# A running minimum over 256 MB on one core: fewer correction passes, doubling steps in the serial middle, smaller pieces at the stage borders

## The chip, the core and the metric

The kernel runs on 1 core of one Trainium2 chip. The metric is device time in microseconds (us), the median over runs. The granted clock in the records is 1.0. A profile is one execution; its span is 1.8 to 2.3 us shorter than the time of the same execution, so stages are compared with stages and times with times.

A few names: HBM is the memory that holds the input and the output, SBUF the one that holds the tiles, with up to 128 partitions in the profile's lines; the profile's DMA lines move data between the two. In the profile PE is the matmul engine TensorE (used here for transposes), DVE is VectorE, ACT is ScalarE, POOL is GpSimd, which issues the gathers and scatters, and SPq is the queue that issues the loads and stores.

## The reference

```python
def setup_inputs():
    return {"x": np.random.randn(8192, 8192).astype(np.float32)}

def reference(x):
    return np.minimum.accumulate(x.flatten()).reshape(x.shape).astype(np.float32)
```

The output is the running minimum over all 67 million values in row order. On random data a new minimum is rare. Cut into 65,536 blocks of 1024 values, only 9 blocks of this draw hold a value below everything before them; every other block of the output is one constant.

## The kernel before

`x` is seen as 64 groups of 128 rows (one row per partition), each row as 8 blocks of 1024. The kernel works in four stages.

1. Load every group (4 MB) and reduce each block to its minimum.
2. In the middle, with no data moving, turn the 65,536 block minima into exclusive prefix minima `pfx`. This is done along the row (8 blocks), across the 128 rows of a group (after a transpose), and across the 64 groups. Each is a "windowed" reduction: an access pattern with overlapping windows, so that 128 results over windows of 128 make 16,384 element reads.
3. ScalarE (ACT) fills 128x1024 pieces with the constant `pfx`, and the tiles are stored. Beside that, the blocks that may hold a new minimum ("candidates", at most 16 per partition, padded with fillers) are gathered from HBM, and VectorE (DVE) scans them.
4. After the last store, the scanned candidate blocks are scattered over the output, 128 blocks at a time.

```python
    NCAND = 16
    ...
    with tc.tile_pool(name="xin", bufs=3) as xpool:
        for g in range(G):
            xt = xpool.tile([P, K, S], f32, tag="x")
            nc.sync.dma_start(out=xt, in_=xg[g])
            nc.vector.tensor_reduce(out=bmpad[:, g, K : 2 * K], in_=xt, axis=AX, op=MIN)
    ...
    win_x = bass.AP(tensor=tpad.tensor, offset=tpad.offset, ap=[tpad.ap[0], [1, P], [1, P]])
    nc.vector.tensor_reduce(out=xgt, in_=win_x, axis=AX, op=MIN)      # one of three windowed minima
    ...
    nc.vector.max(m1, score)                                          # 8 best candidates
    nc.vector.match_replace(out=score2, in_to_replace=m1, in_values=score, imm_value=-1.0)
    nc.vector.max(m2, score2)                                         # 8 more
    ...
    for i in range(NCAND):                                            # prefix of each candidate
        nc.gpsimd.indirect_dma_start(out=pgath[:, i : i + 1], ..., in_=pdram, ...)
    ...
        pwork = fixpool.tile([P, 2 * S], f32)                         # and qwork, with two memsets
        for i in range(NCAND):
            nc.gpsimd.indirect_dma_start(out=pwork[:, S : 2 * S], ..., in_=xflat, ...)
            # ten doubling steps of 128x1024 on VectorE, into fixres[:, i, :]
        for g in range(G):
            ot = opool.tile([P, K, S], f32, tag="o")
            for k in range(K):
                nc.scalar.activation(out=ot[:, k, :], in_=ones_s, ..., scale=pfx[:, g, k : k + 1])
            nc.sync.dma_start(out=og[g], in_=ot)
        for i in range(NCAND):
            nc.gpsimd.indirect_dma_start(out=oflat, ..., in_=fixres[:, i, :], in_offset=None)
```

## Time and profile before

Median 1382.05 us (12 runs, 1381.89 to 1382.38).

| stage | from | to | length, us |
|---|---|---|---|
| load, to the end of the last reduction | 0 | 632.2 | 632.2 |
| middle, to the end of `pfx` | 632.2 | 663.5 | 31.3 |
| stores, to the start of the first scatter | 663.5 | 1319.85 | 656.3 |
| scatters and end | 1319.85 | 1380.3 | 60.5 |

The first view is the windows of the kernel before. Each line gives a stretch in us from the start, its length, the busy time and instruction count of each engine, the clock, the busy share of the DMA engines and their GB/s.

```profile
core 0: us, PE busy (x) PEld busy (x) DVE busy (x) ACT busy (x) POOL busy (x), PEclk, DMA share, GB/s
0.00:623.50 623.50, 0.00 (x0) 0.00 (x0) 547.89 (x67) 0.00 (x0) 3.70 (x12) 1.00 1.00 431
623.50:663.50 40.00, 1.23 (x4) 0.51 (x4) 38.77 (x14) 0.00 (x0) 0.00 (x0) 1.00 0.00 0
663.50:674.00 10.50, 0.00 (x0) 0.00 (x0) 5.09 (x16) 10.40 (x10) 1.76 (x2) 1.00 0.35 25
674.00:1319.00 645.00, 0.00 (x0) 0.00 (x0) 196.92 (x160) 529.17 (x504) 42.44 (x31) 1.00 1.00 429
1319.00:1380.30 61.30, 0.00 (x0) 0.00 (x0) 0.00 (x0) 0.00 (x0) 15.42 (x16) 1.00 0.33 137
```

The two long stretches have the DMA engines fully busy at about 430 GB/s. The three other stretches, 112 us together, have them idle, or busy for about a third. That is where most of the time can be had.

The next view is the timeline around the middle: start, duration, engine, line, operation, and in brackets the idle time before it and what ended it.

```profile
623.50 8.69 DVE L71 TENSOR_REDUCE bmpad<-xt 128x8 f32<-128x8192 f32 x1 [0.98 <-DMA xt<-in_x_dram]
632.82 4.41 DVE L84 TENSOR_REDUCE E<-bmpad 128x512 f32<-128x4096 f32 x1
637.58 0.91 DVE L212 MEMSET pwork<- 128x1024 f32 x1 [0.16 <-issue]
638.42 17.15 DVE L95 TENSOR_REDUCE xgt<-tpad 64x128 f32<-64x16384 f32 x1
656.94 4.41 DVE L107 TENSOR_REDUCE tpf<-tp_pad 1x64 f32<-1x4096 f32 x1
662.83 0.69 DVE L122 TENSOR_TENSOR pfx<-E,rowpre 128x512 f32<-128x512 f32 x1
673.33 62.30 SPq L253 DMA_DIRECT2D out_dram<-ot  x8
```

The last tile's whole 8.69 us reduction comes after its data has landed, and one windowed reduction of 17.15 us is over half of the middle. The first store is issued 9.8 us after `pfx` is done (the last line sums eight store issues; only its start counts here).

The last view is the timeline of the scatters (three of sixteen).

```profile
1319.85 0.99 POOL L256 DMA_INDIRECT out_dram<-fixres,bidx  x1 [179.99 <-DMA out_dram<-ot]
1323.43 0.97 POOL L256 DMA_INDIRECT out_dram<-fixres,bidx  x1 [2.60 <-DMA out_dram<-fixres,bidx]
1327.05 0.96 POOL L256 DMA_INDIRECT out_dram<-fixres,bidx  x1 [2.64 <-DMA out_dram<-fixres,bidx]
```

Each scatter waits for the one before it to land; all write the same tensor. The median gap from start to start is 3.56 us. The last two gaps are 4.05 us; they are about 0.5 us longer than the others, and nothing here tells why.

### The profile page before, as it was taken

Reading aid. Unit: us, or ns where it says so; the run is one execution under the profiler, and the core shown is the slowest. Engines: PE = TensorE matmul, PEld = TensorE weight load, DVE = VectorE, ACT = ScalarE, POOL = GpSimd, SP = SyncE. Lnnn points to the kernel's source line nnn. Section 1 sums busy time; section 2 is a strip of 40 time slices with the busy share of each in tenths; the row PEclk is TensorE's granted clock in tenths of the full one; section 3 lists DMA queues with packets and bytes.
Section 4 is the critical chain, followed back from the end, with each engine's and each line's share of the span. In section 5 each row is a group of like instructions: output and inputs, shape, how many; then the busy total and the mean of one; then the engine's idle time right before and its main releaser. Section 6 shows DMA issues by size and latency. Waiting matters only on the chain.

```text
span 1380.3 us, 1251 instructions
## 1 busy us (share of the span) xinstructions
PE 1.2 (0%) x4; PEld 0.5 (0%) x4; DVE 788.7 (57%) x255; ACT 539.6 (39%) x513; POOL 63.3 (5%) x60
## 2 busy tenths in 40 slices
PE   0000000000000000000000000000000000000000
PEld 0000000000000000000000000000000000000000
DVE  5989889898988889899324333554333553000000
ACT  0000000000000000000798878888888788888500
POOL 1000000000000000000400000001000000000022
DMA  9999999999999999990599999999999999999933
GB/s 410 427 439 428 438 429 437 430 436 432 434 432 433 434 432 436 430 438 4 205 423 436 426 435 431 439 426 439 430 433 430 437 428 438 427 439 427 438 151 137
DMA packets 31770, 554.01 MB, mean 401 GB/s; under 512 B 11280, under 2 KB 11280, under 8 KB 15376
## 3 DMA queue, kind: packets, MB, share of 16 engines
q1 hardware_dynamic: 26640, 537.14, 90.5%
q0 software_dynamic: 5120, 16.79, 3.0%
q14 instruction: 10, 0.08, 0.0%
HBM read 276.83 MB, written 277.09 MB: 401 GB/s over the span
## 4 chain that ended last, share of the span: by engine, by line
DMA 67%; DVE 16%; ACT 15%; issue 2%; POOL 0%; ACTq 0%; POOLq 0%; PE 0%
DMA out_dram<-ot 33%; DMA xt<-in_x_dram 32%; ACT ot L246 15%; DVE bmpad L71 14%; DMA out_dram<-fixres,bidx 2%; DVE xgt L95 1%; POOL out_dram L256 0%; DVE tpf L107 0%; DVE E L84 0%; ACT L246 0%; POOLq L287 0%; ACTq L287 0%; DVE qwork L213 0%; DVE pwork L212 0%; DVE pfx L122 0%
## 5 line engine op out<-in xcount | busy, mean ns | idle before, releaser
L71 DVE TENSOR_REDUCE bmpad<-xt 128x8 f32<-128x8192 f32 x64 | 555.9, 8686 | 74.7 <-DMA xt<-in_x_dram 74.7
L246 ACT ACTIVATE ot<-ones_s,pfx 128x1024 f32<-128x1024 f32 x512 | 538.3, 1134 | 95.3 <-DMA out_dram<-ot 95.3
L235 DVE TENSOR_TENSOR qwork<-pwork 128x1024 f32<-128x1024 f32 x80 | 98.0, 1225 | 299.4 <-DMA pwork<-in_x_dram,bidx 297.2
L246 ACT ACT_TABLE_LOAD x1 | 1.3, 1283 | 663.6 <-DVE pfx L122 663.6
L235 DVE TENSOR_TENSOR pwork<-qwork 128x1024 f32<-128x1024 f32 x64 | 78.4, 1225 | 2.2
L216 POOL DMA_INDIRECT pwork<-in_x_dram,bidx x16 | 28.9, 1805 | 419.2 <-DVE qwork L235 418.9
L199 POOL DMA_INDIRECT pgath<-pdram,bidx x16 | 15.3, 957 | 672.2 <-DMA pdram<-pfx 667.7
L256 POOL DMA_INDIRECT out_dram<-fixres,bidx x16 | 15.4, 964 | 219.9 <-DMA out_dram<-ot 180.0
L226 DVE SCALAR_TENSOR_TENSOR fixres<-qwork,pgath 128x1024 f32<-128x1024 f32 x16 | 20.6, 1285 | 0.6
L95 DVE TENSOR_REDUCE xgt<-tpad 64x128 f32<-64x16384 f32 x1 | 17.2, 17153 | 0.0
L107 DVE TENSOR_REDUCE tpf<-tp_pad 1x64 f32<-1x4096 f32 x1 | 4.4, 4408 | 0.0
L84 DVE TENSOR_REDUCE E<-bmpad 128x512 f32<-128x4096 f32 x1 | 4.4, 4408 | 0.0
L64 DVE MEMSET bmpad<- 128x512 f32 x1 | 0.5, 485 | 0.9 <-PEq L276 0.9
L213 DVE MEMSET qwork<- 128x1024 f32 x1 | 0.9, 912 | 0.2 <-issue 0.2
L212 DVE MEMSET pwork<- 128x1024 f32 x1 | 0.9, 912 | 0.2 <-issue 0.2
L48 POOL MEMSET ones_s<- 128x1024 f32 x1 | 1.0, 956 | 0.0
L87 PE MATMUL mt_ps<-identity,rowmin 128*64 128x128 f32 x1 | 0.4, 392 | 633.0 <-DVE rowmin L76 633.0
L50 POOL IOTA bmap_i<- 128x512 int32 x1 | 0.8, 756 | 0.0
L143 DVE TENSOR_TENSOR score<-sc,sc 128x512 f32<-128x512 f32 x1 | 0.7, 693 | 0.1
L153 DVE MAX8 m<-score 128x8 f32<-128x512 f32 x1 | 0.7, 694 | 0.0
L141 DVE TENSOR_TENSOR sc<-bmpad,pfx 128x512 f32<-128x512 f32 x1 | 0.7, 692 | 0.0
L122 DVE TENSOR_TENSOR pfx<-E,rowpre 128x512 f32<-128x512 f32 x1 | 0.7, 691 | 0.0
(38 smaller groups left out, 9.4 us busy)
## 6 DMA issues: line engine op xcount, KB each, us to landing
xt<-in_x_dram SPq DMA_DIRECT2D x64, 4096.0 KB, 20.3
out_dram<-ot SPq DMA_DIRECT2D x64, 4096.0 KB, 21.7
pdram<-pfx SPq DMA_DIRECT2D x1, 256.0 KB, 7.5
pgath<-pdram,bidx POOLq DMA_INDIRECT x16, 7.9
pwork<-in_x_dram,bidx POOLq DMA_INDIRECT x16, 17.8
out_dram<-fixres,bidx POOLq DMA_INDIRECT x16, 3.3
```

The costliest lines, as they stand in the source:

```text
L48: nc.gpsimd.memset(ones_s, 1.0)
L71: nc.vector.tensor_reduce(out=bmpad[:, g, K : 2 * K], in_=xt, axis=AX, op=MIN)
L84: nc.vector.tensor_reduce(out=E, in_=win_e, axis=AX, op=MIN)
L95: nc.vector.tensor_reduce(out=xgt, in_=win_x, axis=AX, op=MIN)
L107: nc.vector.tensor_reduce(out=tpf, in_=win_t, axis=AX, op=MIN)
L199: nc.gpsimd.indirect_dma_start(out=pgath[:, i : i + 1], out_offset=None, in_=pdram, in_offset=bass.IndirectOffsetOnAxis(ap=bidx[:, i : i + ...
L212: nc.vector.memset(pwork[:, 0:S], FMAX)
L216: nc.gpsimd.indirect_dma_start(out=pwork[:, S : 2 * S], out_offset=None, in_=xflat, in_offset=bass.IndirectOffsetOnAxis(ap=bidx[:, i : i + ...
L226: nc.vector.scalar_tensor_tensor(out=fixres[:, i, :], in0=cur[:, S : 2 * S], scalar=pgath[:, i : i + 1], in1=cur[:, S - d : 2 * S - d], op ...
L235: nc.vector.tensor_tensor(out=nxt[:, S : 2 * S], in0=cur[:, S : 2 * S], in1=cur[:, S - d : 2 * S - d], op=MIN,)
L246: nc.scalar.activation(out=ot[:, k, :], in_=ones_s, func=mybir.ActivationFunctionType.Copy, bias=0.0, scale=pfx[:, g, k : k + 1],)
L256: nc.gpsimd.indirect_dma_start(out=oflat, out_offset=bass.IndirectOffsetOnAxis(ap=bidx[:, i : i + 1], axis=0), in_=fixres[:, i, :], in_off ...
```

## The change

The intent is to shorten the three stretches in which the DMA engines idle, and to halve the correction work. The core of the diff, with cuts marked:

```diff
-    NCAND = 16
+    NCAND = 8
+    pad = small.tile([P, 112], f32)                 # never used
+    nc.gpsimd.memset(pad, 0.0)
 ...
+    pwork = small.tile([P, 2 * S], f32)             # qwork and their memsets too: now before the loads
 ...
-            nc.sync.dma_start(out=xt, in_=xg[g])
-            nc.vector.tensor_reduce(out=bmpad[:, g, K : 2 * K], in_=xt, axis=AX, op=MIN)
+            left = G - g
+            n = 8 if left <= 1 else 4 if left <= 4 else 2 if left <= 9 else 1
+            w = K // n
+            for k in range(0, K, w):
+                nc.sync.dma_start(out=xt[:, k : k + w, :], in_=xg[g, :, k : k + w, :])
+                nc.vector.tensor_reduce(out=bm[:, g, k : k + w], in_=xt[:, k : k + w, :], axis=AX, op=MIN)
 ...
-    nc.vector.tensor_reduce(out=xgt, in_=win_x, axis=AX, op=MIN)      # and the two other windows
+    d = 1
+    while d < P:                                                      # and the two other loops
+        nc.vector.tensor_tensor(out=tdst[:, P : 2 * P], in0=tsrc[:, P : 2 * P],
+                                in1=tsrc[:, P - d : 2 * P - d], op=MIN)
+        tsrc, tdst = tdst, tsrc
+        d *= 2
 ...
-    nc.vector.match_replace(...)                                      # second eight candidates: gone
-    nc.vector.max(m2, score2)
 ...
-            nc.sync.dma_start(out=og[g], in_=ot)
+                if g == 0 and k == K // 2 - 1:                        # first store in two halves
+                    nc.sync.dma_start(out=og[g][:, 0 : K // 2, :], in_=ot[:, 0 : K // 2, :])
+            ...
```

Filler candidates are now real blocks of the partition itself, picked by the sign of the score. The result is right as long as no partition has more than 8 candidates (16 before); this draw has at most 4.

More of the change, by code (lines that the diff above doesn't have):

```diff
@@ L28 @@
     NR, NC = x.shape
-    assert (NR, NC) == (8192, 8192), "kernel is specialised for 8192x8192"
     G = NR // P
@@ L32 @@
     NBLK = NR * K
-    NCAND = 16
+    NCAND = 8
+    GK = G * K
     AX = mybir.AxisListType.X
@@ L43 @@
     psum = ctx.enter_context(tc.tile_pool(name="psum", bufs=1, space=bass.MemoryType.PSUM))
+    dramp = ctx.enter_context(tc.tile_pool(name="dram", bufs=1, space=bass.MemoryType.DRAM))
+    pad = small.tile([P, 112], f32)
+    nc.gpsimd.memset(pad, 0.0)
     identity = small.tile([P, P], f32)
@@ L48 @@
     nc.gpsimd.memset(ones_s, 1.0)
-    bmap_i = small.tile([P, G * K], mybir.dt.int32)
+    bmap_i = small.tile([P, GK], mybir.dt.int32)
     nc.gpsimd.iota(bmap_i, pattern=[[P * K, G], [1, K]], channel_multiplier=K)
-    bmap_f = small.tile([P, G * K], f32)
-    nc.gpsimd.tensor_copy(out=bmap_f, in_=bmap_i)
-    sc1 = small.tile([P, G * K], f32)
+    sc1 = small.tile([P, GK], f32)
+    nc.gpsimd.tensor_copy(out=sc1, in_=bmap_i)
     nc.gpsimd.tensor_scalar(
         out=sc1,
-        in0=bmap_f,
+        in0=sc1,
+        scalar1=-2.0,
+        op0=mybir.AluOpType.mult,
+        scalar2=float(2 * NBLK + 2),
+        op1=mybir.AluOpType.add,
+    )
@@ new lines @@
+    bm = small.tile([P, G, K], f32)
+    tpad = small.tile([G, 2 * P], f32)
+    tqad = small.tile([G, 2 * P], f32)
+    nc.vector.memset(tpad[:, 0 : P + 1], FMAX)
+    nc.vector.memset(tqad[:, 0:P], FMAX)
+    tppad = small.tile([1, 2 * G], f32)
+    tqpad = small.tile([1, 2 * G], f32)
+    nc.vector.memset(tppad[:, 0 : G + 1], FMAX)
+    nc.vector.memset(tqpad[:, 0:G], FMAX)
+    epad = small.tile([P, G, 2 * K], f32)
+    eqad = small.tile([P, G, 2 * K], f32)
+    nc.vector.memset(epad[:, :, 0 : K + 1], FMAX)
@@ new lines @@
+    nc.vector.memset(eqad[:, :, 0:K], FMAX)
+    pwork = small.tile([P, 2 * S], f32)
+    qwork = small.tile([P, 2 * S], f32)
+    nc.vector.memset(pwork[:, 0:S], FMAX)
+    nc.vector.memset(qwork[:, 0:S], FMAX)
+    with tc.tile_pool(name="xin", bufs=3) as xpool:
+        for g in range(G):
+            xt = xpool.tile([P, K, S], f32, tag="x")
+            left = G - g
[3 more added lines that the diff above has]
+                nc.sync.dma_start(out=xt[:, k : k + w, :], in_=xg[g, :, k : k + w, :])
+                nc.vector.tensor_reduce(
+                    out=bm[:, g, k : k + w],
+                    in_=xt[:, k : k + w, :],
+                    axis=AX,
+                    op=MIN,
+                )
@@ new lines @@
+    nc.vector.tensor_copy(out=epad[:, :, K + 1 : 2 * K], in_=bm[:, :, 0 : K - 1])
+    esrc, edst = epad, eqad
+    d = 1
+    while d < K:
+        nc.vector.tensor_tensor(
+            out=edst[:, :, K : 2 * K],
+            in0=esrc[:, :, K : 2 * K],
+            in1=esrc[:, :, K - d : 2 * K - d],
+            op=MIN,
+        )
+        esrc, edst = edst, esrc
+        d *= 2
+    ex = esrc[:, :, K : 2 * K]
+    rowmin = small.tile([P, G], f32)
+    nc.vector.tensor_reduce(out=rowmin, in_=bm, axis=AX, op=MIN)
@@ new lines @@
+    mt_ps = psum.tile([G, P], f32)
+    nc.tensor.transpose(mt_ps, rowmin, identity)
+    nc.vector.tensor_copy(out=tpad[:, P + 1 : 2 * P], in_=mt_ps[:, 0 : P - 1])
+    tsrc, tdst = tpad, tqad
+    d = 1
+    while d < P:
+        nc.vector.tensor_tensor(
+            out=tdst[:, P : 2 * P],
+            in0=tsrc[:, P : 2 * P],
+            in1=tsrc[:, P - d : 2 * P - d],
+            op=MIN,
+        )
+        tsrc, tdst = tdst, tsrc
+        d *= 2
+    tg_t = small.tile([G, 1], f32)
+    nc.vector.tensor_reduce(out=tg_t, in_=mt_ps, axis=AX, op=MIN)
@@ new lines @@
+    t1_ps = psum.tile([1, G], f32)
+    nc.tensor.transpose(t1_ps, tg_t, identity[:G, :G])
+    nc.vector.tensor_copy(out=tppad[:, G + 1 : 2 * G], in_=t1_ps[:, 0 : G - 1])
+    usrc, udst = tppad, tqpad
+    d = 1
+    while d < G:
+        nc.vector.tensor_tensor(
+            out=udst[:, G : 2 * G],
+            in0=usrc[:, G : 2 * G],
+            in1=usrc[:, G - d : 2 * G - d],
+            op=MIN,
+        )
+        usrc, udst = udst, usrc
+        d *= 2
+    tp_ps = psum.tile([G, 1], f32)
@@ new lines @@
+    nc.tensor.transpose(tp_ps, usrc[:, G : 2 * G], identity[:1, :1])
+    rt = small.tile([G, P], f32)
+    nc.vector.tensor_scalar(
+        out=rt, in0=tsrc[:, P : 2 * P], scalar1=tp_ps, scalar2=None, op0=MIN
+    )
+    r_ps = psum.tile([P, G], f32)
+    nc.tensor.transpose(r_ps, rt, identity[:G, :G])
+    pfx = small.tile([P, G, K], f32)
+    nc.vector.tensor_tensor(
+        out=pfx, in0=ex, in1=r_ps[:, :, None].to_broadcast([P, G, K]), op=MIN
+    )
+    score = small.tile([P, GK], f32)
+    nc.vector.tensor_tensor(
+        out=score.rearrange("p (a b) -> p a b", b=K), in0=bm, in1=pfx,
+        op=mybir.AluOpType.is_lt,
+    )
@@ new lines @@
+    nc.vector.scalar_tensor_tensor(
+        out=score,
+        in0=score,
+        scalar=-0.5,
+        in1=sc1,
+        op0=mybir.AluOpType.add,
+        op1=mybir.AluOpType.mult,
+    )
+    m1 = small.tile([P, NCAND], f32)
+    nc.vector.max(m1, score)
+    mneg = small.tile([P, NCAND], f32)
+    nc.vector.tensor_scalar(
+        out=mneg, in0=m1, scalar1=-1.0, scalar2=None, op0=mybir.AluOpType.mult
+    )
+    bidx_f = small.tile([P, NCAND], f32)
+    nc.vector.tensor_tensor(out=bidx_f, in0=m1, in1=mneg, op=mybir.AluOpType.max)
@@ L57 @@
+    nc.vector.tensor_scalar(
+        out=bidx_f,
+        in0=bidx_f,
         scalar1=-1.0,
@@ L61 @@
     )
-    bmpad = small.tile([P, G, 2 * K], f32)
-    nc.vector.memset(bmpad[:, :, 0:K], FMAX)
-    bm = bmpad[:, :, K : 2 * K]
-    with tc.tile_pool(name="xin", bufs=3) as xpool:
-        for g in range(G):
-            xt = xpool.tile([P, K, S], f32, tag="x")
-            nc.sync.dma_start(out=xt, in_=xg[g])
-            nc.vector.tensor_reduce(
-                out=bmpad[:, g, K : 2 * K], in_=xt, axis=AX, op=MIN
-            )
-    rowmin = small.tile([P, G], f32)
-    nc.vector.tensor_reduce(out=rowmin, in_=bm, axis=AX, op=MIN)
@@ L78 @@
-    E = small.tile([P, G, K], f32)
-    win_e = bass.AP(
-        tensor=bmpad.tensor,
-        offset=bmpad.offset,
-        ap=[bmpad.ap[0], [2 * K, G], [1, K], [1, K]],
-    )
-    nc.vector.tensor_reduce(out=E, in_=win_e, axis=AX, op=MIN)
-    mt_ps = psum.tile([G, P], f32)
-    nc.tensor.transpose(mt_ps, rowmin, identity)
-    tpad = small.tile([G, 2 * P], f32)
-    nc.vector.memset(tpad[:, 0:P], FMAX)
-    nc.vector.tensor_copy(out=tpad[:, P : 2 * P], in_=mt_ps)
-    xgt = small.tile([G, P], f32)
@@ L92 @@
-    win_x = bass.AP(
-        tensor=tpad.tensor, offset=tpad.offset, ap=[tpad.ap[0], [1, P], [1, P]]
-    )
-    nc.vector.tensor_reduce(out=xgt, in_=win_x, axis=AX, op=MIN)
-    tg = small.tile([G, 1], f32)
-    nc.vector.tensor_reduce(out=tg, in_=tpad[:, P : 2 * P], axis=AX, op=MIN)
-    t1_ps = psum.tile([1, G], f32)
-    nc.tensor.transpose(t1_ps, tg, identity[:G, :G])
-    tp_pad = small.tile([1, 2 * G], f32)
-    nc.vector.memset(tp_pad[:, 0:G], FMAX)
-    nc.vector.tensor_copy(out=tp_pad[:, G : 2 * G], in_=t1_ps)
@@ L103 @@
-    tpf = small.tile([1, G], f32)
-    win_t = bass.AP(
-        tensor=tp_pad.tensor, offset=tp_pad.offset, ap=[tp_pad.ap[0], [1, G], [1, G]]
-    )
-    nc.vector.tensor_reduce(out=tpf, in_=win_t, axis=AX, op=MIN)
-    tp_ps = psum.tile([G, 1], f32)
-    nc.tensor.transpose(tp_ps, tpf, identity[:1, :1])
-    tpcol = small.tile([G, 1], f32)
-    nc.vector.tensor_copy(out=tpcol, in_=tp_ps)
-    rt = small.tile([G, P], f32)
-    nc.vector.tensor_scalar(
-        out=rt, in0=xgt, scalar1=tpcol, scalar2=None, op0=MIN
-    )
@@ L116 @@
-    r_ps = psum.tile([P, G], f32)
-    nc.tensor.transpose(r_ps, rt, identity[:G, :G])
-    rowpre = small.tile([P, G], f32)
-    nc.vector.tensor_copy(out=rowpre, in_=r_ps)
-    pfx = small.tile([P, G, K], f32)
-    nc.vector.tensor_tensor(
-        out=pfx, in0=E, in1=rowpre[:, :, None].to_broadcast([P, G, K]), op=MIN
-    )
-    if "fix" in DEBUG_DISABLE:
-        with tc.tile_pool(name="outp", bufs=3) as opool:
-            for g in range(G):
-                ot = opool.tile([P, K, S], f32, tag="o")
-                for k in range(K):
-                    nc.scalar.activation(
-                        out=ot[:, k, :],
-                        in_=ones_s,
-                        func=mybir.ActivationFunctionType.Copy,
-                        bias=0.0,
-                        scale=pfx[:, g, k : k + 1],
-                    )
-                nc.sync.dma_start(out=og[g], in_=ot)
-        return
@@ L140 @@
-    sc = small.tile([P, G, K], f32)
-    nc.vector.tensor_tensor(out=sc, in0=bm, in1=pfx, op=mybir.AluOpType.is_lt)
-    score = small.tile([P, G * K], f32)
-    nc.vector.tensor_tensor(
-        out=score.rearrange("p (a b) -> p a b", b=K),
-        in0=sc,
-        in1=sc1.rearrange("p (a b) -> p a b", b=K),
-        op=mybir.AluOpType.mult,
-    )
-    nc.vector.tensor_scalar(
-        out=score, in0=score, scalar1=-1.0, scalar2=None, op0=mybir.AluOpType.add
-    )
-    m1 = small.tile([P, 8], f32)
@@ L153 @@
-    nc.vector.max(m1, score)
-    score2 = small.tile([P, G * K], f32)
-    nc.vector.match_replace(out=score2, in_to_replace=m1, in_values=score, imm_value=-1.0)
-    m2 = small.tile([P, 8], f32)
-    nc.vector.max(m2, score2)
-    mm = small.tile([P, NCAND], f32)
-    nc.vector.tensor_copy(out=mm[:, 0:8], in_=m1)
-    nc.vector.tensor_copy(out=mm[:, 8:16], in_=m2)
-    bidx_f = small.tile([P, NCAND], f32)
-    nc.vector.tensor_scalar(
-        out=bidx_f,
-        in0=mm,
-        scalar1=-1.0,
-        op0=mybir.AluOpType.mult,
-        scalar2=float(NBLK),
-        op1=mybir.AluOpType.add,
-    )
@@ L170 @@
-    padmap_i = small.tile([P, NCAND], mybir.dt.int32)
-    nc.gpsimd.iota(padmap_i, pattern=[[1, NCAND]], channel_multiplier=NCAND)
-    padmap = small.tile([P, NCAND], f32)
-    nc.gpsimd.tensor_copy(out=padmap, in_=padmap_i)
-    valid = small.tile([P, NCAND], f32)
-    nc.vector.tensor_scalar(
-        out=valid, in0=mm, scalar1=0.0, scalar2=None, op0=mybir.AluOpType.is_gt
-    )
-    bidx_v = small.tile([P, NCAND], f32)
-    nc.vector.tensor_tensor(
-        out=bidx_v, in0=bidx_f, in1=padmap, op=mybir.AluOpType.subtract
-    )
@@ L182 @@
-    nc.vector.tensor_tensor(
-        out=bidx_v, in0=bidx_v, in1=valid, op=mybir.AluOpType.mult
-    )
-    nc.vector.tensor_tensor(
-        out=bidx_v, in0=bidx_v, in1=padmap, op=mybir.AluOpType.add
-    )
     bidx = small.tile([P, NCAND], mybir.dt.uint32)
-    nc.vector.tensor_copy(out=bidx, in_=bidx_v)
-    dramp = ctx.enter_context(tc.tile_pool(name="dram", bufs=1, space=bass.MemoryType.DRAM))
+    nc.vector.tensor_copy(out=bidx, in_=bidx_f)
     pdram = dramp.tile([NBLK, 1], f32)
-    pdram_bpk = bass.AP(
-        tensor=pdram.tensor, offset=0, ap=[[K, P], [P * K, G], [1, K]]
-    )
+    pdram_bpk = bass.AP(tensor=pdram.tensor, offset=0, ap=[[K, P], [P * K, G], [1, K]])
@@ L209 @@
         fixres = fixpool.tile([P, NCAND, S], f32)
-        pwork = fixpool.tile([P, 2 * S], f32)
-        qwork = fixpool.tile([P, 2 * S], f32)
-        nc.vector.memset(pwork[:, 0:S], FMAX)
-        nc.vector.memset(qwork[:, 0:S], FMAX)
         nsteps = (S - 1).bit_length()
@@ L252 @@
                 )
-            nc.sync.dma_start(out=og[g], in_=ot)
+                if g == 0 and k == K // 2 - 1:
+                    nc.sync.dma_start(
+                        out=og[g][:, 0 : K // 2, :], in_=ot[:, 0 : K // 2, :]
+                    )
+            if g == 0:
+                nc.sync.dma_start(
+                    out=og[g][:, K // 2 : K, :], in_=ot[:, K // 2 : K, :]
+                )
+            else:
+                nc.sync.dma_start(out=og[g], in_=ot)
         for i in range(NCAND):
```

## The prediction

> **What bounds the kernel now.** By the 40 slices and the windows, DMA engines are busy at 433 GB/s for 591 us of loading and from about 674 to 1319 us of storing. The chain of waits shows the rest in three stretches:
> 1. Load tail and serial middle. The last tile lands at 623.5 us; VectorE reduces it (8.69 us), then the small steps run alone until pfx is done at 663.5 us. DMA share from 624 to 664 us is 0.00. The middle after the last reduction is 31.3 us; three windowed reductions take 17.15, 4.41 and 4.41 us of it.
> 2. The first store is issued at 673.3 us, after a table load and eight 1.05 us activations.
> 3. After the last store (1319 us) 16 scatters run strictly one after another, 3.56 us from start to start, 58 us. [...] the trace has 3.3 us. It is latency, so the number of scatters counts.
> Inside the store stage, a tile costs 10.15 us while gathers run and 9.70 us after: over 45 tiles that is 20 us for the gathers, about 1.3 us each.
>
> **What the change does, costed.**
> - Last nine tiles loaded and reduced in pieces. The last reduction is then 1024 elements, about 1.2 us (estimate: 0.96 elements/ns plus 0.15 us, from the 512- and 8192-element reductions), and the epad copy runs just before it. Saves about 7.0 us; smaller descriptors give back about 0.5 us.
> - Windowed minima become doubling steps. A windowed reduction touches 16384 elements for 128 results[...]. In its place: four 128x512-size steps (0.7 us each), seven of 128 (about 0.3) and six of 64 elements (about 0.2), the two memsets moved to the start, two PSUM copies gone. I add up 9.5 us for the middle, against 31.3: saves 21.8 us.
> - First store in halves: issued about 4 us sooner, but it queues behind the pfx store (7.5 us to landing), and tile 1 is not ready earlier. ACT makes a tile in 8.43 us, DMA takes 9.7, so at most 1.3 us is gained; say 1.5 us with the first gather filling the gap.
> - 8 candidates, not 16: scatters 8 x 3.56 = 28.5 us saved; gathers 8 x 1.3 = 10.5 us saved in the store stage. The 98 us of VectorE work saved lies beside the stores: nothing.
> - The fewer candidate instructions (match-replace and so on) are off the chain: pfx already releases ACT. The pad tile: nothing.
>
> **Sum.** 7.0 - 0.5 + 21.8 + 1.5 + 10.5 + 28.5 = 68.8 us. Predicted 1313 us, range 1306 to 1322. Faster by over 2%: 0.97; within 2%: 0.02; slower: 0.01.
>
> **What would show it.** Last load lands at 623 to 625 us; pfx ends near 635 us; the DMA hole shrinks from 50 to about 20 us; eight gathers, the tiles after them still at 9.7 us; the last store lands near 1278 us; eight scatters still 3.5 us apart; bulk reductions still 8.69 us and store rate still 433 GB/s.
>
> **What would make it wrong.** Pieces of 4 KB per partition loading clearly slower; small dependent VectorE steps costing 0.4 us or more (thirteen of them: 3 us); the padded gathers and scatters, which now hit blocks 32 KB apart instead of 64 KB, running at another rate; the half store idling the DMA queue between tiles 0 and 1 and gaining nothing.

The scatters are eight times the 3.56 us of the trace, and the middle is its measured 31.3 us less the 9.5 added up. The 3.3 us is the median time of a scatter from issue to landing; that most of it does not go with the bytes was shown only later (2.7 us with half the bytes in a_halfrow, 2.1 with next to none in a_skip_al). The 0.5 us for smaller descriptors and the 0.2 us for the first gather were guesses; a_whole gave 1.2 us for the first, and no run takes the second alone. The short steps, put at about 0.3 and 0.2 us, took 0.27 and 0.21 us in the changed kernel's trace. That the half store queues behind the `pfx` store is not shown by a trace; what it gained was measured, 1.6 us (a_nohalf).

## The result

Median 1308.95 us (8 runs, 1308.80 to 1309.27) against 1382.05 us (12 runs). The ratio is 0.9471, with a 95% interval of 0.9461 to 0.948. A ratio here is the mean time of one kernel's fast runs over that of the other's of the same rounds, so it is not quite the ratio of the medians quoted. The prediction of 1313 us lay inside its range and 4 us too high.

The windows of the changed kernel, cut near its own stage borders (1272.0 to 1275.9 us, from the end of the stores to the first scatter, is left out):

```profile
0.00:624.90 624.90, 0.00 (x0) 0.00 (x0) 559.26 (x93) 0.00 (x0) 3.66 (x11) 1.00 1.00 430
624.90:633.50 8.60, 1.23 (x4) 0.51 (x4) 7.71 (x24) 0.00 (x0) 0.00 (x0) 1.00 0.00 0
633.50:641.00 7.50, 0.00 (x0) 0.00 (x0) 2.76 (x7) 7.44 (x7) 1.15 (x1) 1.00 0.65 66
641.00:1272.00 631.00, 0.00 (x0) 0.00 (x0) 98.48 (x80) 531.93 (x507) 20.60 (x15) 1.00 1.00 432
1275.90:1306.80 30.90, 0.00 (x0) 0.00 (x0) 0.00 (x0) 0.00 (x0) 7.71 (x8) 1.00 0.33 136
```

The stretch with no data moving went from 40 to 8.6 us, and the scatters from 61 to 31 us. The timeline shows what stands there now:

```profile
624.68 0.39 DVE L98 COPY epad<-bm 128x448 f32<-128x448 f32 x1
624.99 1.21 DVE L91 TENSOR_REDUCE bm<-xt 128x1 f32<-128x1024 f32 x1
629.83 0.27 DVE L120 TENSOR_TENSOR tpad<-tqad 64x128 f32<-64x128 f32 x1
630.03 0.21 DVE L136 TENSOR_TENSOR tqpad<-tppad 1x64 f32<-1x64 f32 x1
630.17 0.27 DVE L120 TENSOR_TENSOR tqad<-tpad 64x128 f32<-64x128 f32 x1
632.79 0.69 DVE L154 TENSOR_TENSOR pfx<-eqad,r_ps 128x512 f32<-128x512 f32 x1 [0.46 <-PE r_ps L151]
639.13 0.35 SPq L246 DMA_DIRECT2D out_dram<-ot  x1
1275.88 0.99 POOL L257 DMA_INDIRECT out_dram<-fixres,bidx  x1 [451.76 <-DMA out_dram<-ot]
1279.46 0.97 POOL L257 DMA_INDIRECT out_dram<-fixres,bidx  x1 [2.59 <-DMA out_dram<-fixres,bidx]
```

The last reduction takes 1.21 us, the windowed reductions are gone, and the scatters are still about 3.56 us apart (3.54 to 3.60; the last two gaps are again longer, 4.04 and 4.03). A second sight: the steps of two chains (L120, L136) alternate, and each starts before the one ahead of it has ended.

The chain of waits of the changed kernel is of no use; it breaks off after three pieces at the very end. The stage borders had to be read from the timeline.

| stage | before | after | measured gain | predicted gain |
|---|---|---|---|---|
| load, to the end of the last reduction | 632.2 | 626.2 | 6.0 | 7.0 - 0.5 = 6.5 |
| middle | 31.3 | 7.3 | 24.0 | 21.8 |
| stores, to the first scatter | 656.3 | 642.4 | 13.9 | 1.5 + 10.5 = 12.0 |
| scatters and end | 60.5 | 31.0 | 29.4 | 28.5 |
| sum | | | 73.4 | 68.8 |

### The profile page after: what moved, and what is told of

Read it like the earlier page. It is cut to its first block, busy times and chain, and to the rows that moved or that the text cites. A ratio compares the mean times of both kernels' runs of the same rounds, so it can differ in the third digit from the quotient of the medians.

```text
span 1306.9 us, 1185 instructions
## 1 busy us (share of the span) xinstructions
PE 1.2 (0%) x4; PEld 0.5 (0%) x4; DVE 668.2 (51%) x203; ACT 539.4 (41%) x513; POOL 33.1 (3%) x35
## 5 line engine op out<-in xcount | busy, mean ns | idle before, releaser
L91 DVE TENSOR_REDUCE bm<-xt 128x8 f32<-128x8192 f32 (+3 forms) x85 | 557.0, 6575 | 64.3 <-DMA xt<-in_x_dram 64.2
L227 DVE TENSOR_TENSOR qwork<-pwork 128x1024 f32<-128x1024 f32 x40 | 49.0, 1226 | 116.6 <-DMA pwork<-in_x_dram,bidx 115.5
L227 DVE TENSOR_TENSOR pwork<-qwork 128x1024 f32<-128x1024 f32 x32 | 39.2, 1224 | 1.1
L208 POOL DMA_INDIRECT pwork<-in_x_dram,bidx x8 | 14.2, 1774 | 792.6 <-DVE bidx L188 632.5
L257 POOL DMA_INDIRECT out_dram<-fixres,bidx x8 | 7.7, 966 | 470.9 <-DMA out_dram<-ot 451.8
L218 DVE SCALAR_TENSOR_TENSOR fixres<-qwork,pgath 128x1024 f32<-128x1024 f32 x8 | 10.3, 1284 | 0.3
L195 POOL DMA_INDIRECT pgath<-pdram,bidx x8 | 7.6, 944 | 5.4 <-DMA pdram<-pfx 3.3
L120 DVE TENSOR_TENSOR tqad<-tpad 64x128 f32<-64x128 f32 x4 | 1.1, 276 | 0.0
L120 DVE TENSOR_TENSOR tpad<-tqad 64x128 f32<-64x128 f32 x3 | 0.8, 271 | 0.0
```

The costliest lines, as they stand in the source:

```text
L91: nc.vector.tensor_reduce(out=bm[:, g, k : k + w], in_=xt[:, k : k + w, :], axis=AX, op=MIN,)
L120: nc.vector.tensor_tensor(out=tdst[:, P : 2 * P], in0=tsrc[:, P : 2 * P], in1=tsrc[:, P - d : 2 * P - d], op=MIN,)
L195: nc.gpsimd.indirect_dma_start(out=pgath[:, i : i + 1], out_offset=None, in_=pdram, in_offset=bass.IndirectOffsetOnAxis(ap=bidx[:, i : i + ...
L208: nc.gpsimd.indirect_dma_start(out=pwork[:, S : 2 * S], out_offset=None, in_=xflat, in_offset=bass.IndirectOffsetOnAxis(ap=bidx[:, i : i + ...
L218: nc.vector.scalar_tensor_tensor(out=fixres[:, i, :], in0=cur[:, S : 2 * S], scalar=pgath[:, i : i + 1], in1=cur[:, S - d : 2 * S - d], op ...
L227: nc.vector.tensor_tensor(out=nxt[:, S : 2 * S], in0=cur[:, S : 2 * S], in1=cur[:, S - d : 2 * S - d], op=MIN,)
```

## The experiments

Twelve kernels were run. The stage lengths below are read from each run's timeline as in the table above. The length of a DMA packet is the mean over all packets of a size in the trace's packet records. The start addresses of tiles come from the memory allocation of the built program; no trace shows them. The experiments ran on three chips, on which the kernel before took 1382.14, 1382.04 and 1381.99 us, so a difference of some us between two runs is not one of chips.

### The candidates alone (b_cand8)

```diff
 # kernel before
-    NCAND = 16
+    NCAND = 8
-    score2 = ...; match_replace(...); m2 = ...; max(m2, score2); mm = [m1, m2]
+    mm = m1
```

> The kernel before with 8 candidates in place of 16 and nothing else changed (second maximum and match-replace removed). Theory (each scatter is a round trip of fixed length, each gather takes DMA time from the stores): eight scatters fewer at 3.56 us is 28.5 us, eight gathers fewer at about 1.3 us is 10.5 us, so 1343 us; scatter spacing stays 3.5 to 3.6 us; store stage about 10.5 us shorter. Rival (the scatters cost their bytes: 524 KB at 433 GB/s is 1.2 us each): about 10 us from the scatters and 10 from the gathers, 1362 us.

Measured: 1347.47 us, 4.5 us more than the theory, and 14.5 us less than the rival. The scatters were about right: eight, 3.59 to 3.63 us apart before the last two. What was off shows first in a stage that has nothing to do with candidates. The load stage ended at 634.25 us, where the kernel before has 632.19, although its code is the same. Its 32 KB packets had a mean of 1219.0 ns, against 1215.1 before. The only thing that I could see reaching the load is placement: the smaller index tiles let the big tiles start elsewhere in SBUF, at 192 modulo 1024 bytes instead of 512.

### The spacer alone (a_nopad)

```diff
 # changed kernel
-    pad = small.tile([P, 112], f32)
-    nc.gpsimd.memset(pad, 0.0)
```

> The changed kernel without the unused 448-byte pad tile, so that every later tile sits 448 bytes lower. Theory: nothing, 1309 us within 1 us, every stage within 0.5 us. Rival: the placement matters, to ACT, to the reductions or to the DMA rate, and part of the 4 us that the change gained over the prediction comes from it: over 1310.5 us.

Measured: 1314.24 us (1313.71 to 1314.93), 5.3 us slower (4.7 in the profiled executions). The rival holds. The load ended 2.6 us later (628.79), the store stage was 1.9 us longer (644.32), and the middle was the same 7.28 us. The windows in mid-load and mid-store of the changed kernel:

```profile
100.00:540.00 440.00, 0.00 (x0) 0.00 (x0) 394.42 (x46) 0.00 (x0) 0.00 (x0) 1.00 1.00 433
860.00:1240.00 380.00, 0.00 (x0) 0.00 (x0) 0.00 (x0) 329.30 (x314) 0.00 (x0) 1.00 1.00 433
```

and the same two of the kernel without the spacer:

```profile
100.00:540.00 440.00, 0.00 (x0) 0.00 (x0) 392.64 (x46) 0.00 (x0) 0.00 (x0) 1.00 1.00 431
860.00:1240.00 380.00, 0.00 (x0) 0.00 (x0) 0.00 (x0) 328.28 (x313) 0.00 (x0) 1.00 1.00 431
```

DMA is fully busy in all four and moves 431 instead of 433 GB/s. The load and store tiles start at 576 modulo 1024 without the spacer and at 0 with it. A 32 KB packet took 1218.5 instead of 1215.1 ns, a 16 KB one 614.2 instead of 611.1, an 8 KB one 313.7 instead of 309.0, a 4 KB one of the loads 162.8 instead of 159.0. So it is 3 to 5 ns per packet in the mean, not in proportion to its size. It is not one fixed price: with the spacer 7,006 of the 7,040 load packets of 32 KB took exactly 1213 ns, without it 996 did and most others took 1214 to 1222; of the store packets about half still took 1213. Each of the 16 engines moves eight 32 KB packets per tile. Over the 55 tiles loaded whole that makes 440 x 3.4 ns = 1.5 us, and the smaller packets of the last nine tiles (80, 96 and 64 per engine at 3.1, 4.7 and 3.8 ns) make another 0.9 us; the measured loss was 2.6.

### Where the border lies (a_128)

```diff
 # changed kernel: big tiles start at 128 modulo 1024
-    pad = small.tile([P, 112], f32)
+    pad = small.tile([P, 144], f32)
```

> The changed kernel with the spacer 128 bytes longer, so that the large tiles start at a multiple of 128 but not of 256 bytes. Theory[...]: as slow as without the spacer, 1314 us, 32 KB packets at a mean of 1218 ns. Rival A (a 64-byte or finer rule: what matters is a multiple of 128): 1309 us, 1215 ns. Rival B (the rule is only 512 or 1024): also 1314 us, which the next run tells apart.

Measured: 1314.49 us, and 1218.6 ns per 32 KB packet. A start at 128 modulo 1024 is as slow as one at 576, so rival A falls. With the other runs, the next one among them, this fits a border at multiples of 256 bytes. The 32 KB packets had a mean of 1219.1 (a_window), 1218.5 (a_nopad), 1218.6 and 1219.0 ns (b_cand8) with the tiles 32, 64, 128 and 192 bytes past such a multiple (at 544, 576, 128 and 192 modulo 1024), and of 1214.7 to 1215.1 ns at 0, 256 and 512. Between the changed kernel and a_nopad or a_128 only starts in SBUF differ. So the runs fit that border, and show a mean cost of 3 to 5 ns per packet that grows neither with the size nor with the offset; what causes it is not shown.

### The windows (a_window, then a_window_256)

```diff
 # changed kernel: the three doubling loops back to the windowed reductions of before (with their small copies out of PSUM)
-    while d < P: nc.vector.tensor_tensor(...)         # three loops
+    nc.vector.tensor_reduce(out=xgt, in_=win_x, axis=AX, op=MIN)   # three windows
 # a_window_256 only: big tiles at 256 modulo 1024 (544 in the first run)
-    pad = small.tile([P, 112], f32)
+    pad = small.tile([P, 40], f32)
```

> The changed kernel with its three doubling minima put back to the windowed reductions of before, all else as changed (the two large memsets stay at the start). Theory: the middle stage, from the end of the last reduction of loaded data to the end of pfx, goes from 7.3 us to about 29 us (31.3 us in the kernel before, less two memsets of about 1.05 us), so the time is 1309 + 22 = 1331 us, and no other stage changes. Rival: a part of the 24 us that the middle lost came from the earlier end of the loads or from copies removed, not from the windows; then the time is under 1326 us.

Measured: 1337.92 us, 7 us over the theory; in the first run the theory could not be told from a cost of placement. (A memset takes 0.91 us in the trace of the kernel before, 1.07 with the idle time before it.)

> The changed kernel with windowed reductions again, its spacer now set so that the large tiles start at a multiple of 256 but not of 512 bytes (they started at 544 modulo 1024 in the first run of it). Theory (256 is enough): packets at 1215 ns, the load 2.6 and the store stage 1.9 us shorter than in the first run, time 1337.9 - 4.5 = 1333.4 us; that leaves 24.4 us for windows against doubling, of which about 4.4 us is the first windowed reduction, which the scheduler put before the last small reduction of loaded data. Rival (512 is needed): 1338 us and 1218 ns again.

Measured: 1332.07 us, and 1215.0 ns per 32 KB packet, so 256 is enough. The windows, with the small copies that belong to them, cost 23.1 us against doubling. They are seen in two places: the middle is 26.2 us instead of 7.3, and the load stage ends 3.9 us later, because the scheduler put the first windowed reduction ahead of the last small reduction. In the first run the timeline reads:

```profile
627.77 4.42 DVE L97 TENSOR_REDUCE E<-bmpad 128x512 f32<-128x4096 f32 x1
632.11 1.21 DVE L81 TENSOR_REDUCE bmpad<-xt 128x1 f32<-128x1024 f32 x1
634.94 17.21 DVE L108 TENSOR_REDUCE xgt<-tpad 64x128 f32<-64x16384 f32 x1
```

### Two chains, not interleaved (a_serial)

```diff
 # changed kernel: the second chain needs the end of the first
-    nc.vector.tensor_reduce(out=tg_t, in_=mt_ps, axis=AX, op=MIN)
+    nc.vector.tensor_tensor(out=tg_t, in0=tsrc[:, 2 * P - 1 : 2 * P], in1=mt_ps[:, P - 1 : P], op=MIN)
```

> The changed kernel with one step altered so that its two short chains of doubling minima (seven steps over 128 elements, six over 64) cannot be interleaved: the minimum of a row is taken from the end of the first chain, so the second chain starts only after it. One VectorE step is added and a reduction removed. Theory: part of why the middle took 7.3 us and not the 9.5 us predicted is that four of the six short steps hide in the gaps between dependent steps of the other chain; taken apart, the middle grows by 1.0 to 2.0 us, time about 1310.5 us. Rival: a step's own duration was over-estimated and order does not matter: middle within 0.4 us of 7.3 us.

Measured: 1310.61 us; the middle is 8.72 us, 1.4 us longer. The steps in order (the first two of the first chain, what lies between the chains, and the first two of the second):

```profile
628.74 0.28 DVE L120 TENSOR_TENSOR tqad<-tpad 64x128 f32<-64x128 f32 x1
629.05 0.28 DVE L120 TENSOR_TENSOR tpad<-tqad 64x128 f32<-64x128 f32 x1
630.95 0.15 DVE L129 TENSOR_TENSOR tg_t<-tqad,mt_ps 64x1 f32<-64x1 f32 x1
631.46 0.21 DVE L134 COPY tppad<-t_ps 1x63 f32<-1x63 f32 x1 [0.35 <-PE t_ps L133]
631.70 0.22 DVE L138 TENSOR_TENSOR tqpad<-tppad 1x64 f32<-1x64 f32 x1
631.95 0.21 DVE L138 TENSOR_TENSOR tppad<-tqpad 1x64 f32<-1x64 f32 x1
```

A dependent step of the first chain starts 0.31 us after the one before it, one of the second 0.25 us. In the changed kernel a pair, one of each, takes 0.34 us (629.83 to 630.17). So the second chain's step is nearly free there; four such pairs make 4 x (0.31 + 0.25 - 0.34) = 0.9 us. The rest of the 1.4 us is by this working not a matter of the steps: the row minimum, its transpose and its copy (630.95 to 631.70), which lie beside the first chain in the changed kernel, now stand between the chains. I had added all thirteen steps up.

### The last tiles whole (a_whole)

```diff
 # changed kernel
-            n = 8 if left <= 1 else 4 if left <= 4 else 2 if left <= 9 else 1
+            n = 1
```

> The changed kernel with the last nine tiles loaded and reduced whole again. Theory: the last load lands at about 623.5 us, a little earlier than in pieces, but its reduction then takes 8.69 us where it took 1.2 us; last reduction ends at about 632.2 us in place of 626.2, time 1309 + 6 = 1315 us. Rival: the pieces cost the load stage as much as they save at its end; then within 1 us of 1309 us.

Measured: 1315.68 us, 6.7 us slower: the last reduction ends at 632.27 instead of 626.20, and the middle is 0.5 us longer: the `epad` copy (0.39 us), which ran ahead of the last reduction, now comes after it, and the steps behind it stand in another order. A 4 KB packet takes 159.0 ns, an eighth of a 32 KB packet 151.9. Summed over the pieces of the nine tiles (64 x 159.0, 96 x 309.0 and 80 x 611.1 ns per engine in place of 72 x 1215) the smaller packets cost 1.2 us; I had said 0.5.

### The first store whole (a_nohalf)

```diff
 # changed kernel
-                if g == 0 and k == K // 2 - 1: (store the first half)
-            ...
+            nc.sync.dma_start(out=og[g], in_=ot)
```

> The changed kernel with the first store whole again, issued after eight activations. Theory of the prediction: tile 1 is not ready earlier (activations 8.43 us a tile, DMA 9.7 us), so the half store gains only the difference, 1.3 us: 1310.3 us. Rival A: the store stage is shifted by the whole 4.2 us that the first half is issued earlier: 1313 us. Rival B: the pfx store in the same queue and a gap before tile 1 eat it all: 1309 us.

Measured: 1310.48 us; the store stage is 1.6 us longer (643.97). The half store gains what the prediction said, not the 4.2 us by which it is issued earlier.

### Candidates without the placement (b_cand8_al)

```diff
 # kernel before, 8 candidates, big tiles back at 512 modulo 1024
+    pad = small.tile([P, 80], f32)
+    nc.gpsimd.memset(pad, 0.0)
```

> The kernel before with 8 candidates, now with a 320-byte spacer so that its large tiles start at the same place modulo 1024 (512) as in the kernel before. New theory (a start that is not a multiple of 256 bytes costs each DMA packet about 3.4 ns, which is what made the first 8-candidate run 4.3 us slower than forecast): 32 KB packets back at a mean of 1215 ns, not 1218, load stage back to 632.2 us, time 1343 us. Rival (the candidates are worth only 34.7 us and placement has nothing to do with it): 1347.5 us again.

Measured: 1342.09 us, with 1214.7 ns per 32 KB packet and the load stage back at 632.20 us. Eight candidates less are worth 39.9 us: 11.3 us in the store stage (645.03 against 656.33) and 29.0 us at the end. The spacer alone took back 5.4 us of the first candidate run.

### Four candidates (a_cand4)

```diff
 # changed kernel; correct for this draw only
-    NCAND = 8
+    NCAND = 4                     # the first four of the eight maxima
```

> The changed kernel with 4 candidates per partition in place of 8. It is correct for this data (no partition has more than four) but not in general. Theory (cost per candidate: 3.56 us of scatter and about 1.3 us of gather): 1309 - 4 x 4.86 = 1289.5 us. Rival: a gather costs only its bytes at full rate, 1.2 us, or the tiny gathers of the prefix count as well: between 1288 and 1290.5 us, told by the length of the store stage; the gathers are free: 1294.7 us.

Measured: 1288.76 us, correct on this data. The store stage is 5.2 us shorter, 1.3 us for each gather pair (a block and its prefix).

### Half the bytes of a scatter (a_halfrow)

```diff
 # changed kernel; wrong on purpose
-                out=oflat,  ... ap=bidx[:, i : i + 1] ... in_=fixres[:, i, :],
+                out=oflat2, ... ap=bidx2[:, i : i + 1] ... in_=fixres[:, i, 0 : S // 2],
```

> The changed kernel, wrong on purpose: each scatter writes only the first half (2 KB) of every block, so the bytes of a scatter are halved and the count is the same; the second half of blocks that hold a new minimum is then wrong. Theory (fixed round trip plus bytes at full rate): spacing of the scatters falls by 0.6 us, from 3.56 to about 2.95 us, time about 1304 us. Pure count: spacing unchanged, 1309 us. Pure bytes: spacing halves to 1.8 us, 1295 us.

Measured: 1309.63 us, a wrong result. The total missed: the two added index tiles moved the big tiles to 64 modulo 1024, and the load and store stages grew by 2.5 and 1.9 us. The scatters themselves did what the theory said:

```profile
1283.26 0.99 POOL L264 DMA_INDIRECT out_dram<-fixres,bidx  x1 [2.02 <-DMA out_dram<-fixres,bidx]
1286.28 0.97 POOL L264 DMA_INDIRECT out_dram<-fixres,bidx  x1 [2.04 <-DMA out_dram<-fixres,bidx]
```

They start 3.0 us apart instead of 3.56: 256 KB is worth 0.56 us. Taking the other 256 KB off too would leave about 2.4 us (an estimate at the same rate); the next run tests it.

### Fillers skipped (a_skip_al)

```diff
 # changed kernel: a filler's index is out of range, and the bounds check skips it
-    mneg = ...; bidx_f = max(m1, mneg); bidx_f = -bidx_f + (NBLK + 1)
+    bidx_f = -m1 + (NBLK + 1)                 # a filler (m1 < 0) comes out above NBLK
+            bounds_check=NBLK - 1, oob_is_err=False,      # on all three indirect DMAs
-    pad = small.tile([P, 112], f32)
+    pad = small.tile([P, 120], f32)           # keeps the big tiles at 0 modulo 1024
+    (memset of pgath, and of all of pwork instead of half)
```

> A version meant to be faster: the changed kernel with the filler candidates given an index out of range, so that the bounds check of the indirect DMAs skips them; gathers and scatters keep their number but move only the blocks that hold a new minimum (9 of 1024). Large tiles at 0 modulo 1024. Theory (a scatter is a fixed round trip plus its bytes; from the half-row run, 0.6 us per 256 KB): spacing 3.56 - 1.2 = about 2.35 us, 8 of them 9.5 us less; the gathers stop taking 1.2 us each from the stores, another 9 us; time about 1291 us. Rival (skipping costs as much as writing, the length is a pure count): spacing 3.56 us, gain only from the gathers, 1300 us; or none, 1309 us.

Measured: 1290.28 us, correct, ratio to the kernel before 0.9336 (0.9323 to 0.9349). It beats both kernels, with the same limit of 8 candidates per partition as the changed one. The store stage is 9.0 us shorter, and the scatters are about 2.3 us apart (2.33 to 2.43, with a first gap of 2.68 and last two of 2.86 and 2.84). The packet records show 18 block moves of 4 KB by the gathers and scatters, so just the 9 blocks were read and written:

```profile
1274.24 0.97 POOL L255 DMA_INDIRECT out_dram<-fixres,bidx  x1 [1.38 <-DMA out_dram<-fixres,bidx]
1276.58 0.97 POOL L255 DMA_INDIRECT out_dram<-fixres,bidx  x1 [1.37 <-DMA out_dram<-fixres,bidx]
```

From issue to landing a scatter takes 2.1 us with next to no bytes, 2.7 with 256 KB and 3.3 with 512 KB.

## Why the prediction was right, point by point

- **Scatters count by number.** Right. Half the bytes saved only 0.56 of 3.56 us each, half the number saved half the stage. Predicted 28.5 us, measured 29.0 alone and 29.4 in the whole change. The last 0.5 to 0.9 us lie after the last scatter's start (6.0 us before, 5.5 with eight candidates, 5.1 after the change); no run tells why.
- **Gathers take DMA time from the stores.** Right in kind; the term "10.5 us" measured 11.3 us alone. With the fillers skipped (a_skip_al) the store stage gave back 9.0 us for eight gathers, so most of the cost goes with the bytes.
- **First store in halves.** Right: 1.5 us said, 1.6 measured by taking it away.
- **Store stage as a whole.** 13.9 us, of which 11.3 + 1.6 = 12.9 are accounted for by those two runs. The last 1.0 us stays open. The block gather now starts at 636.85 us, before any store, and may fill the gap there; no run took that alone away.
- **Last tiles in pieces.** Right: 6.5 us said, 6.0 seen in the load stage, and 6.7 of total time lost without it. The term "about 0.5 us" for smaller packets was too small: 1.2 us from the packet times.
- **Windows into doubling steps.** Right in mechanism: taking doubling away cost 23.1 us. The mis-sized term of the sum is "I add up 9.5 us for the middle"; it measured 7.3. 1.4 of the 2.2 us are the overlap of two independent chains and of the transpose between them, which I had added as if serial. The rest is consistent with independent 128x512 steps starting 0.6 us apart (626.12 and 626.72 in the changed kernel's timeline) where I took 0.7, but no run isolates it.
- **"The pad tile: nothing".** This step failed, though the sum did not suffer: that is luck, since the sum had no term for placement, and in both kernels the big tiles start at a multiple of 256. Without the spacer the changed kernel is 5.3 us slower. The spacer gains nothing over the kernel before, whose big tiles happened to start at a multiple of 512. It prevents a loss that the other edits would have caused by shifting everything allocated after them. I had not thought of placement at all, and four of my first experiments (b_cand8, a_nopad, a_window, a_halfrow) missed by 4 to 7 us, mostly for it, before I looked at addresses.

The stages gained 4.6 us more than the sum: the middle 2.2, the store stage 1.9 and the end 0.9, less 0.5 in the load (4.5 after rounding). In the times it is 4.3 us, since the two profiled spans differ by 73.4 us and the medians by 73.1.

## What to carry to other kernels

Price the stretches in which the bound resource idles first; there a step can cost its full length (here the windows lengthened the middle and the load by 18.9 + 3.9 = 22.8 us, and the time by 23.1), and a chain of dependent transfers can cost its round trips more than its bytes (here, at 512 KB each, 2.1 of 3.3 us). When a stage is DMA-bound, any edit that adds or removes a small tile can move the big buffers in SBUF, which cost about 5 us of 1309 here (slow at 64, 128, 192, 544 and 576 modulo 1024, not at 0, 256 and 512); look at start addresses and at the time of single packets before comparing two kernels that differ in allocations. Look whether independent chains of small steps will be interleaved before adding them up: here a pair of steps took 0.34 us, not 0.56.
